# Even mixer of a hybrid encoder: when queries, keys and weight splits are asked for

## The chip, the cores and the metric

The kernel runs on one core of one Trainium2 chip. The metric is the device time of one execution in microseconds (us). Before the change three runs gave 937.4, 937.48 and 937.48 us, median 937.48.

## What is computed

The reference is a bidirectional encoder of two layers over 256 tokens (a grid of 4 rows of 64) with 1024 channels, all in float32. Each layer adds half a SwiGLU feed-forward (1024 to 2816 and back), then a mixer, then half a second feed-forward; a last RMSNorm ends it. The change lies in the mixer of the even layer:

```python
def even_mixer(h, w_in, q_gain, k_gain, sink, w_out, rope1, rope_axial):
    proj = h @ w_in            # 1024 -> qa 512, ka 128, va 128, qb 512, kb 128, vb 128
    ...
    qa = apply_axial_rope(rms_norm(qa, q_gain), *rope_axial)
    ka = apply_axial_rope(rms_norm(ka, k_gain), *rope_axial)
    oa = global_gqa(qa, ka, va)
    qb = apply_rope(qb, *rope1)
    kb = apply_rope(kb, *rope1)
    ob = windowed_gqa_sink(qb, kb, vb, sink)
    return jnp.concatenate([oa, ob], axis=-1) @ w_out
```

Group a is 8 global heads with 2 key heads, whose queries and keys are RMS-normalised per head; group b is 8 windowed heads (128 tokens to each side) with 2 key heads and a sink logit per head. A head has 64 channels.

## The kernel before, in words

**Products in split float32.** TensorE multiplies in a reduced float format (FP32R). To keep precision the kernel writes each factor as a high and a low part. ScalarE rounds a value to its high part (`high_part`, L482), VectorE subtracts it from the value for the low part (`low_part`, L485), and a product of a 128 x 128 block of activations with a 128 x 512 piece of weights is three matmuls: high by high (L474), high by low (L475) and low by high (L476). Weights come from HBM as raw tiles through SyncE's DMA queue (L382); a raw tile is cut into splits of two pieces each.

**What sets the order.** Every engine runs its instructions in the order in which the program issues them. The program counts in products: after each one it calls `tick`. A tick first issues the low part of the piece whose high part was issued last (`low`), then advances the tasks, in the order in which they were started, and last adds the stage's rate to the counter `due`; when `due` reaches the size of the next split step (1 for this stage's narrow pieces, 2 for the wide pieces of the feed-forward), that high part is issued (`supply`) and the size is taken off. A product whose piece isn't split yet has it split on the spot, high and low (`mm`). A task is a Python generator: `yield n` means that it goes on n ticks later. All the lists of waits and rates at the head of the file are such counts. `EVEN_RATE` gives 0.38, 0.48, 0.48, 0.48 and 0.5 pieces per product for the five parts of the even mixer. `due` is set anew only near the end of each feed-forward (`ENDS`).

**The even mixer** works on two blocks of 128 tokens (`tt` 0 and 1) and has 80 products: 16 for keys and values of both groups, 16 for group b's queries, 16 for group a's queries, and 16 for each half of the output projection, b first. In each part block 0 has the first eight. It uses 40 narrow pieces, eight per part, each for both blocks.

**Keys** (`keys`): a tick after a block's projection ScalarE copies keys and values out of PSUM; group a's keys are normalised on VectorE and GpSimd; GpSimd rotates them; `KB_WAIT` ticks later TensorE transposes them (L1206) into a bank of the pool `tp`, which has two; a tick later ScalarE takes their high part (kTaz, kTbz), and another tick later VectorE the low part (kTax, kTbx, beside a copy of the high part on GpSimd, L594).

**Queries** (`queries`): a tick after the projection VectorE rotates them out of PSUM (L1142 or L1144, then L1157); for group b three ticks later (`ROPE_WAIT`), for group a nine ticks later (`QA_WAIT`), TensorE transposes them (L552) into a `tp` bank; a tick later `stack_q` issues the two halves' high parts on ScalarE, and another tick later their low parts on VectorE. The odd layer's mixer calls `stack_q` too.

**Attention** (`attend`): one task goes through the head pairs of group b, then of group a. It starts a pair when the query task of its block and the key tasks have ended. A pair issues its scores on TensorE at once (L1068, L1069, and for group b L1072, a mask), and later, by `EVEN_WAITS`, the row maximum on VectorE, the exponentials on ScalarE (L1108), sum and reciprocal on VectorE, the scaling on GpSimd (L1122), transposes (L1130) and the product with the values (L1053) on TensorE. Until the first pair starts the task asks in each tick; between pairs it waits `EVEN_GAP` ticks.

Of the kernel before, what the change touches and what calls it, by code (L numbers as in the profile page):

```python
# [62 lines left out]
NAT_WAIT = 2  # L63
ROPE_WAIT = [3, 3]
KB_WAIT = {
    "a": [8, 7],
    "b": [8, 9],
}
KA_WAITS = [[1, 6], [0, 5]]
QA_WAIT = [9, 9]  # L70
ROWS, ROWS_WAIT = 4, 30
BIAS_WAIT, BIAS_GAP = 4, [0, 3]
EVEN_GAP = {
# [135 lines left out]
class Trunk:  # L209
# [88 lines left out]
    def plan(self):  # L298
# [65 lines left out]

        yield from ffn("ffn1", 0, 0)
        yield from even()
        yield from ffn("ffn2", 0, 2)
        yield from ffn("ffn1", 1, 3)
# [204 lines left out]
        self.low_part(flat(lo), tb[:, : n * P], flat(hi))  # L573
        dest += [(hi[:, i, :], lo[:, i, :]) for i in range(n)]

    def stack_q(self, tb, tag, bufs, dest):


        X = [self.t([P, 4 * P], f"{tag}{s}", bufs, F32R) for s in range(2)]
        for s in range(2):  # L580
            self.high_part(X[s][HALF[s]], tb[HALF[s]])
        yield 1
        for s in range(2):
            self.low_part(X[s][HALF[1 - s]], tb[HALF[s]], X[s][HALF[s]])
        dest += [[X[s][:, b * P : b * P + P] for s in range(2)] for b in range(4)]
# [587 lines left out]
    def even(self, sink):  # L1173
        nc = self.nc
        rates = iter(EVEN_RATE)
        flat = lambda t: t.rearrange("p a b -> p (a b)")
        tab = {
            "a": [[self.gtab[:, tt, i, :] for i in range(4)] for tt in range(NT)],
            "b": [[self.tab[:, tt, i, :] for i in (4, 5, 2, 3)] for tt in range(NT)],
        }  # L1180
        axial = {"a": 2, "b": 1}
        kT = {g: self.keys_tiles([P, T], f"kT{g}") for g in "ab"}
        vv = {g: [self.t([P, P], f"v{g}{tt}") for tt in range(NT)] for g in "ab"}
        qT = {g: [[], []] for g in "ab"}
        oT = {g: [[], []] for g in "ab"}
        by = [None, None]
        made = {"a": [], "b": []}

        def keys(g, tt, ps):
            yield 1  # L1190
            r = self.rstd_of(tt)
            o = 256 if g == "b" else 0
            k = self.t([P, 2, HD], f"k{g}", 2)
            kr = self.t([P, 2, HD], f"kr{g}", 2)
            nc.scalar.activation(flat(k), ps[:, o : o + P], AF.Copy, scale=r)
            nc.scalar.activation(vv[g][tt], ps[:, o + P : o + 2 * P], AF.Copy, scale=r)
            if g == "a":
                sq = self.squares(k, 2, 1.0)
                yield KA_WAITS[tt][0]
                n = self.head_rstd(sq, 2)  # L1200
                nc.gpsimd.tensor_tensor(k, k, n.unsqueeze(2).to_broadcast([P, 2, HD]), op=ALU.mult)
                yield KA_WAITS[tt][1]
            self.rope(nc.gpsimd, kr, k, 2, axial[g], *tab[g][tt][2:])
            yield KB_WAIT[g][tt]
            tb = self.bank("tp")
            nc.tensor.transpose(tb[:, :P], flat(kr), self.ident)  # L1206
            yield 1
            at = slice(tt * P, tt * P + P)
            yield from self.stack_k(tb[:, :P], *([t[:, at] for t in tiles] for tiles in kT[g]))

        def queries(g, tt, ps):
            yield 1
            r = self.now.r[tt]
            x = ps.rearrange("p (a b) -> p a b", a=8)
            qr = self.t([P, 4, 2, HD], "qr", 2)
            if g == "a":

                sq = self.squares(x, 8, r)
                self.rope(nc.vector, qr, x, 8, axial[g], *tab[g][tt][:2])
                yield QA_WAIT[tt]  # L1220
                n = self.head_rstd(sq, 8)
                by[tt] = self.little([P, 8], f"by{tt}")
                nc.gpsimd.tensor_scalar(by[tt], n, r, 1.0, op0=ALU.mult, op1=ALU.mult)
            else:
                self.rope(nc.vector, qr, x, 8, axial[g], *tab[g][tt][:2], r)
                yield ROPE_WAIT[tt]
            tb = self.turned(qr.rearrange("p j s d -> p (j s d)"))
            yield 1
            yield from self.stack_q(tb, f"qT{g}{tt}", 1, qT[g][tt])

        def heads(g):
            return self.attend(
                lambda tt: qT[g][tt],
                lambda tt, b0: len(made[g]) > 2 + tt and all(task[1] is None for task in made[g][: 3 + tt]),
                lambda b: kT[g],
                lambda b, s, kc: vv[g][kc][:, s * HD : s * HD + HD],
                lambda: True,
                f"oT{g}",
                oT[g],
                EVEN_GAP[g],  # L1240
                EVEN_WAITS[g],
                nc.gpsimd,
                sink=sink if g == "b" else None,
                scale=(lambda tt, b, s: by[tt][:, s * 4 + b : s * 4 + b + 2]) if g == "a" else None,
            )

        def both():
            yield from heads("b")
            yield from heads("a")


        self.rate = next(rates)
        W = self.take(KD)
        for tt in range(NT):
            ps = self.project(self.ready(tt), W, "s")
            for g in "ba":
                made[g].append(self.start(keys(g, tt, ps)))
        attention = None
        for g in "ba":
            self.rate = next(rates)  # L1260
            W = self.take(KD)
            for tt in range(NT):
                ps = self.project(self.now.hT[tt], W, "pj")
                made[g].append(self.start(queries(g, tt, ps)))
                if attention is None:
                    attention = self.start(both())
        self.out_proj([oT["b"], oT["a"]], attention, rates)
# [311 lines left out]
```

## Time and profile before

The profile is one execution, taken by the hardware profiler.

| | before |
|---|---|
| median of 3 runs | 937.48 us |
| the profiled execution's own time | 937.71 us |
| its span in the trace | 935.5 us |
| TensorE (PE) busy | 921.9 us (99%), 4405 matmuls |
| VectorE (DVE) busy | 773.4 us (83%) |
| ScalarE (ACT) busy | 675.4 us (72%) |
| GpSimd (POOL) busy | 92.5 us (10%) |
| DMA | 183.14 MB, mean 196 GB/s |

How to read a row of a timeline: start in us, duration in us, engine, line of the program, operation, tile written <- tiles read, shape of what is written and read, and how many instructions were merged (x3). In brackets stands the idle time of the engine just before, if any, and what ended it. PEld is the loading of weights into TensorE, which overlaps its matmuls. In this stage `tp` is a bank for transposes, `pj` one for projections, `s` one for scores; `raw` are weights, `hi` and `lo` their parts; `kra` and `krb` are rotated keys, `qr` rotated queries, `qTa` and `qTb` their transposed parts, `th` and `tl` the parts of the transposed activations.

### The profile page before, as it was taken

Reading aid. Unit: us, or ns where it says so; the run is one execution under the profiler, and the core shown is the slowest. Engines: PE = TensorE matmul, PEld = TensorE weight load, DVE = VectorE, ACT = ScalarE, POOL = GpSimd, SP = SyncE. Lnnn points to the kernel's source line nnn. Section 1 sums busy time; section 2 is a strip of 40 time slices with the busy share of each in tenths; the row PEclk is TensorE's granted clock in tenths of the full one; section 3 lists DMA queues with packets and bytes.
Section 4 is the critical chain, followed back from the end, with each engine's and each line's share of the span. In section 5 each row is a group of like instructions: output and inputs, shape, how many; then the busy total and the mean of one; then the engine's idle time right before and its main releaser. Section 6 shows DMA issues by size and latency. Waiting matters only on the chain.

```text
span 935.5 us, 12377 instructions
## 1 busy us (share of the span) xinstructions
PE 921.9 (99%) x4405; PEld 754.6 (81%) x4405; DVE 773.4 (83%) x1198; ACT 675.4 (72%) x1084; POOL 92.5 (10%) x152
## 2 busy tenths in 40 slices
PE   9999999999999999999999999999999999999997
PEld 6887888877778888888788888888878888888885
DVE  6799679778868889798988888978867696977998
ACT  7678876467777778875657879647777586778853
POOL 1300000064420000000100000008030000000001
PEclk9999999999999999999999999999999999999999
DMA  8858865654327577865466787666424367588651
GB/s 298 281 172 258 245 211 189 212 149 105 108 92 240 179 221 237 254 208 208 159 206 199 225 265 220 224 212 192 162 96 156 110 201 227 166 263 252 167 212 54
DMA packets 129341, 183.14 MB, mean 196 GB/s; under 512 B 50688, under 2 KB 63744, under 8 KB 129280
## 3 DMA queue, kind: packets, MB, share of 16 engines
q1 hardware_dynamic: 128704, 181.58, 61.6%
q10 hardware_dynamic: 576, 0.79, 0.2%
q8 instruction: 34, 0.56, 0.2%
q14 instruction: 27, 0.22, 0.1%
HBM read 169.76 MB, written 1.05 MB: 183 GB/s over the span
## 4 chain that ended last, share of the span: by engine, by line
PE 85%; DVE 8%; ACT 4%; issue 2%; DMA 1%; POOL 0%; POOLq 0%; ACTq 0%; DVEq 0%
PE s L475 12%; PE s L476 12%; PE s L474 12%; PE pj L474 11%; PE pj L475 11%; PE pj L476 11%; DVE lo L485 3%; PE o L475 2%; PE o L474 2%; PE o L476 2%; PE o L1053 2%; PE tp L1130 1%; ACT hi L482 1%; PE tp L530 1%; ACT shi L482 1%
## 5 line engine op out<-in xcount | busy, mean ns | idle before, releaser
L485 DVE TENSOR_TENSOR lo<-raw,hi 128x1024 fp32r<-128x1024 f32 (+1 forms) x372 | 377.9, 1034 | 83.6 <-ACT hi L482 81.8
L482 ACT ACTIVATE hi<-raw 128x1024 fp32r<-128x1024 f32 (+1 forms) x372 | 320.2, 892 | 54.0 <-PE pj L476 11.8
L474 PE MATMUL s<-hi,th 128*128 128x512 f32 x378 | 148.2, 392 | 0.0
L475 PE MATMUL s<-lo,th 128*128 128x512 f32 x378 | 147.4, 390 | 0.1
L476 PE MATMUL s<-hi,tl 128*128 128x512 f32 x378 | 147.3, 390 | 0.0
L474 PE MATMUL pj<-hi,th 128*128 128x512 f32 x366 | 146.2, 400 | 0.0
L475 PE MATMUL pj<-lo,th 128*128 128x512 f32 x366 | 143.3, 392 | 0.6 <-DVE lo L485 0.4
L476 PE MATMUL pj<-hi,tl 128*128 128x512 f32 x366 | 142.9, 390 | 0.0
L475 PEld LDWEIGHTS s<-lo,th 128*128 128x128 f32 x378 | 71.0, 188 | 15.0 <-DVE lo L485 0.7
L476 PEld LDWEIGHTS s<-hi,tl 128*128 128x128 f32 x378 | 71.0, 188 | 14.9
L474 PEld LDWEIGHTS s<-hi,th 128*128 128x128 f32 x378 | 71.1, 188 | 14.4
L475 PEld LDWEIGHTS pj<-lo,th 128*128 128x128 f32 x366 | 68.9, 188 | 15.1 <-DVE lo L485 2.6
L476 PEld LDWEIGHTS pj<-hi,tl 128*128 128x128 f32 x366 | 68.7, 188 | 14.5
L474 PEld LDWEIGHTS pj<-hi,th 128*128 128x128 f32 x366 | 68.9, 188 | 14.1 <-issue 1.0
L494 POOL TENSOR_TENSOR rstd<-var,mhalf 128x1 f32<-128x1 f32 (+2 forms) x16 | 17.1, 1070 | 588.3 <-ACT th L515 309.6
L563 ACT COPY turned<-glu 128x1024 uint16<-128x1024 uint16 (+1 forms) x48 | 60.1, 1252 | 11.5 <-DMA glu<-turned 11.5
L559 ACT COPY turned<-glu 128x1024 uint16<-128x1024 uint16 (+1 forms) x48 | 46.3, 965 | 23.6 <-DVE glu L797 15.6
L482 ACT ACTIVATE shi<-raw 128x1024 fp32r<-128x1024 f32 x28 | 29.7, 1059 | 40.1 <-DVE raw L398 21.3
L474 PE MATMUL s<-hi,g_h 128*128 128x512 f32 (+1 forms) x134 | 52.5, 392 | 0.0
L476 PE MATMUL s<-hi,g_l 128*128 128x512 f32 (+1 forms) x134 | 52.0, 388 | 0.0
L475 PE MATMUL s<-lo,g_h 128*128 128x512 f32 (+1 forms) x134 | 51.9, 388 | 0.0
L482 ACT ACTIVATE shi<-two 128x1024 fp32r<-128x1024 f32 x28 | 29.6, 1057 | 20.9 <-DVE two L398 20.9
(350 smaller groups left out, 1658.1 us busy)
## 6 DMA issues: line engine op xcount, KB each, us to landing
raw<-in_ffn_w_down SPq DMA_DIRECT2D x44, 1024.0 KB, 5.1
raw<-in_ffn_w_up SPq DMA_DIRECT2D x28, 1024.0 KB, 5.2
raw<-in_ffn_w_gate SPq DMA_DIRECT2D x26, 1024.0 KB, 5.2
raw<-in_ffn_w_gate SPq DMA_DIRECT2D x35, 512.0 KB, 4.1
raw<-in_ffn_w_up SPq DMA_DIRECT2D x32, 512.0 KB, 5.3
raw<-in_odd_w_qkv SPq DMA_DIRECT2D x12, 1024.0 KB, 5.2
raw<-in_even_w_in SPq DMA_DIRECT2D x4, 1024.0 KB, 5.0
raw<-in_even_w_out SPq DMA_DIRECT2D x8, 512.0 KB, 5.8
```

Source lines behind the costliest of these rows:

```text
L474: mm(ps, h, wh, start=first, stop=False)
L475: mm(ps, h, wl, start=False, stop=False)
L476: mm(ps, l, wh, start=False, stop=last)
L482: self.nc.scalar.activation(hi, src, AF.Copy)
L485: self.nc.vector.tensor_tensor(lo, src, hi.bitcast(F32), op=ALU.subtract)
L494: nc.gpsimd.tensor_tensor(r[:, :n], v[:, :n], self.mhalf[:, :n], op=ALU.pow)
L530: nc.tensor.transpose(tb[:, j * P : (j + 1) * P], self.x[tt][:, b * P : (b + 1) * P], self.ident)
L559: self.nc.scalar.copy(planes.rearrange("p (h c) -> p h c", h=2), back.rearrange("p (c h) -> p h c", h=2))
L563: self.nc.scalar.copy(planes.rearrange("p (c h) -> p h c", h=2), back.rearrange("p (h c) -> p h c", h=2))
L1053: self.nc.tensor.matmul(O[64 * s : 64 * s + 64, i * P : i * P + P], v(b0 + i, s, kc), pT[s][:, i, kc, :], start=(kc == 0), stop=(kc == 1),)
L1130: nc.tensor.transpose(tb[:, o : o + P], p[:, i, kc * P : kc * P + P], self.ident)
```

## The change

Three things change, all in the even mixer.

- `KB_WAIT["a"][0]` goes from 8 to 6: the transposes of the first block's normalised keys are issued behind the sixth product of group b's queries rather than behind the eighth.
- `stack_q` gets an argument for the wait between high and low part. The even mixer's queries pass 0, so both parts are issued in one tick, for both groups and both blocks, and the query task ends one tick sooner. The odd layer keeps the wait of 1.
- Ahead of the first product of group b's queries 2 is taken off `due`, so that two pieces' splits are withheld there.

```diff
@@ -63,11 +63,12 @@
 KB_WAIT = {
-    "a": [8, 7],
+    "a": [6, 7],
     "b": [8, 9],
 }
 KA_WAITS = [[1, 6], [0, 5]]
 QA_WAIT = [9, 9]
+Q_HOLD = 2
@@ -573,13 +574,14 @@
-    def stack_q(self, tb, tag, bufs, dest):
+    def stack_q(self, tb, tag, bufs, dest, wait=1):
 
         X = [self.t([P, 4 * P], f"{tag}{s}", bufs, F32R) for s in range(2)]
         for s in range(2):
             self.high_part(X[s][HALF[s]], tb[HALF[s]])
-        yield 1
+        if wait:
+            yield wait
         for s in range(2):
             self.low_part(X[s][HALF[1 - s]], tb[HALF[s]], X[s][HALF[s]])
@@ -1226,7 +1228,7 @@
-            yield from self.stack_q(tb, f"qT{g}{tt}", 1, qT[g][tt])
+            yield from self.stack_q(tb, f"qT{g}{tt}", 1, qT[g][tt], 0)
@@ -1260,6 +1262,8 @@
             for tt in range(NT):
+                if g == "b" and tt == 0:
+                    self.due -= Q_HOLD
                 ps = self.project(self.now.hT[tt], W, "pj")
                 made[g].append(self.start(queries(g, tt, ps)))
```

## The prediction, made before the change was timed

> **What bounds the kernel now.** I read the page first, then TensorE's waits by stretch, then the timelines of TensorE, VectorE, ScalarE and GpSimd from 160 to 300 us.
>
> ```profile
> span 935.5 us, 12377 instructions
> PE 921.9 (99%) x4405; PEld 754.6 (81%) x4405; DVE 773.4 (83%) x1198; ACT 675.4 (72%) x1084; POOL 92.5 (10%) x152
> ```
>
> TensorE is idle for only 935.5 - 921.9 = 13.6 us. What a change can give is some of these waits; what it can take is any new wait of TensorE, which nothing later gives back. The stage around the edit, the even mixer, holds three waits that matter. I name its products (three matmuls each) by order: q0 to q15 project the windowed heads' queries, a0 to a15 the global heads' queries, w0 to w15 and v0 to v15 are the two halves of the output projection, f0 on are the next feed-forward's gates. S0 to S7 are the windowed heads' score groups. First wait: the transposes of the queries of the first 128 tokens (L552), behind q11.
>
> ```profile
> 207.46 0.63 PE L552 MATMUL tp<-mats,qr 128*128 128x128 f32 x4 [0.69 <-DVE kTax L485]
> ```
> ```profile
> 202.00 2.19 DVE L485 TENSOR_TENSOR lo<-raw,hi 128x512 fp32r<-128x512 f32 x3
> 204.21 1.53 DVE L1144 SCALAR_TENSOR_TENSOR t<-pj,rstd,tab 128x512 f32<-128x512 f32 x3
> 205.78 1.03 DVE L1157 TENSOR_TENSOR qr<-t,t 128x256 f32<-128x256 f32 x2
> 206.73 0.58 DVE L485 TENSOR_TENSOR kTax<-tp,kTaz 64x128 fp32r<-64x128 f32 x2
> 207.34 0.70 DVE L485 TENSOR_TENSOR lo<-raw,hi 128x512 fp32r<-128x512 f32 x1
> 208.07 0.59 DVE L485 TENSOR_TENSOR kTbx<-tp,kTbz 64x128 fp32r<-64x128 f32 x2
> 208.69 0.69 DVE L485 TENSOR_TENSOR lo<-raw,hi 128x512 fp32r<-128x512 f32 x1
> 209.41 1.41 DVE L485 TENSOR_TENSOR qTb<-tp,qTb 64x512 fp32r<-64x512 f32 x2
> ```
>
> VectorE's queue is the cause: the rotated queries (qr) are done at 206.81, but their transposes need the bank that kTax reads until 207.31, and kTax stands behind the rotation. Second wait, 0.57 us at S0 for the queries' low part; third, 0.94 us at S4:
>
> ```profile
> 207.84 0.47 PE L474 MATMUL pj<-hi,th 128*128 128x512 f32 x1
> ...
> 208.61 0.40 PE L474 MATMUL pj<-hi,th 128*128 128x512 f32 x1
> ...
> 209.30 0.27 PE L1206 MATMUL tp<-mats,kra 128*128 128x128 f32 x1
> 210.15 0.39 PE L1068 MATMUL s<-kTbz,qTb 128*128 128x256 f32 x1 [0.57 <-DVE qTb L485]
> ...
> 221.34 0.36 PE L1068 MATMUL s<-kTbz,qTb 128*128 128x256 f32 x1 [0.94 <-ACT p L1108]
> ```
> ```profile
> 219.78 0.69 DVE L485 TENSOR_TENSOR lo<-raw,hi 128x512 fp32r<-128x512 f32 x1 [0.19 <-ACT hi L482]
> 220.50 1.41 DVE L485 TENSOR_TENSOR qTb<-tp,qTb 64x512 fp32r<-64x512 f32 x2
> ```
>
> The last row's first half (0.69 to 0.70) ends at 221.2, so S4 waits for the second query block's low part as much as for the named exponentials. All three waits together are 2.20 us: that is the ceiling of any gain, 0.23%, just over the 0.2% (1.9 us) that a measurement of this kernel can tell from no change.
>
> **The change part by part.** *The withheld splits* are the part that reaches furthest, so first how far ahead of need the weights are split. The narrow weight pieces of this stage (hi on ScalarE, lo on VectorE) number 40, eight for each of keys and values, q, a, w and v. ScalarE has done 15 of them by q0, the last three here, and the 40th here:
>
> ```profile
> 194.13 1.72 ACT L482 ACTIVATE hi<-raw 128x512 fp32r<-128x512 f32 x3
> ...
> 263.10 0.62 ACT L482 ACTIVATE hi<-raw 128x512 fp32r<-128x512 f32 x1
> ```
>
> With 0.48 due per product (0.5 in v), and the order of hi among ScalarE's other instructions, the remaining 25 are asked for behind q1, q3, ... q15, a1, a4, a6, ... a14, w0, w2, ... w10, w13, w15, v1, v3; no other starting remainder than 0.28 to 0.40 gives that order. Taking 2 from the due drops q1 and q3 and leaves all other places, so from then on each place serves the piece two further back. The counter is not refilled before the next feed-forward's end. Today a piece comes four products or more ahead of its use in the tight spots. After, the list of needs meets the list of places so: the last piece of a (a7) comes behind a6; the pieces of w2, w3 and w7 behind w0, w2 and w6; that of v2 behind v1; and v3's would come behind v3 itself, so the product asks for it on the spot. The work of one piece, hi then lo, is about 1.3 us (0.62 and 0.69 by the rows above) against 0.69 for a product (208.61 to 209.30), so a lead of one or two products is not enough when ScalarE or VectorE has something else in its queue. What it costs goes by the times at which these places now deliver, since both engines are led by TensorE's attention work there:
>
> ```profile
> 222.22 0.67 DVE L485 TENSOR_TENSOR lo<-raw,hi 128x512 fp32r<-128x512 f32 x1
> ...
> 239.40 0.69 DVE L485 TENSOR_TENSOR lo<-raw,hi 128x512 fp32r<-128x512 f32 x1
> ...
> 241.13 0.68 DVE L485 TENSOR_TENSOR lo<-raw,hi 128x512 fp32r<-128x512 f32 x1
> ...
> 263.13 0.69 DVE L485 TENSOR_TENSOR lo<-raw,hi 128x512 fp32r<-128x512 f32 x1
> ...
> 280.03 1.22 DVE L485 TENSOR_TENSOR lo<-raw,hi 128x1024 fp32r<-128x1024 f32 x1
> ...
> 283.06 1.23 DVE L485 TENSOR_TENSOR lo<-raw,hi 128x1024 fp32r<-128x1024 f32 x1
> ```
> ```profile
> 222.36 0.39 PE L475 MATMUL pj<-lo,th 128*128 128x512 f32 x1
> ...
> 239.13 0.39 PE L475 MATMUL pj<-lo,oTb00h 128*128 128x512 f32 x1
> ...
> 240.26 0.39 PE L475 MATMUL pj<-lo,oTb00h 128*128 128x512 f32 x1
> ...
> 263.28 0.39 PE L475 MATMUL pj<-lo,oTa00h 128*128 128x512 f32 x1
> ...
> 280.23 0.39 PE L475 MATMUL s<-lo,th 128*128 128x512 f32 x1
> ...
> 282.05 0.39 PE L475 MATMUL s<-lo,th 128*128 128x512 f32 x1
> ```
>
> These are the second matmuls of a7, w2, w3, v3, f4 and f6, which read lo.
> - a7: its lo would end at 222.89, 0.53 after the need. +0.6 (0 if the shift of VectorE's queue hides it, 1.2 if a6 waits too).
> - w2 and w3: 240.09 against 239.13 is 0.96; 241.81 against 240.26 is 1.55, the larger, which contains the first. For the global heads' queries the low part (1.41 by the row of the same shape) now also moves ahead of w3's lo. +2.0, between 0.2 (VectorE ahead by its two withheld lo, 1.4) and 3.0 (1.55 + 1.41). w7 is then covered by that delay.
> - v2 and v3: the lo behind v1 ends at 263.82; v3's own, asked for on the spot, follows it with 0.7, so 264.5 against 263.28, 1.2; a head's low part may stand between. +1.5, between 0.3 and 2.5.
> - f: v3's extra call catches up one unit of due, the other stays missing, so the wide pieces come about one place late: f4's lo where now the 280.03 row is, f6's where the 283.06 row is, ending at 281.25 and 284.29 against 280.23 and 282.05, that is 1.0 and 2.2. +1.7, between 0.5 and 2.4.
>
> What withholding gives: two lo of the row with x3 (0.73 each) no longer stand ahead of the rotation at 204.21. But q7, whose result the rotation reads, ends no sooner than the transpose behind it now starts:
>
> ```profile
> 203.62 0.27 PE L1206 MATMUL tp<-mats,kra 128*128 128x128 f32 x1
> ```
>
> And the next lo, whose hi now stands behind the keys' kTaz on ScalarE (the transpose two products of 0.69 ahead of 203.62, at 202.3, then kTaz to about 203.1 and hi to 203.7), ends near 204.4. So I let the rotation start at 204.4, not sooner than today. *The keys' transposes*, two products earlier, put kTax ahead of the rotation too; nothing stands behind it that is harmed, its 0.58 fits into VectorE's freed time, and q6 and q7 only move behind a transpose that was on TensorE anyway. GpSimd's two kTax copies move along. Together: qr ends at 204.4 + 2.6 = 207.0, the transposes start at 207.1 in place of 207.46. -0.35 (between -0.69 and 0).
>
> On GpSimd there is a rule to weigh. VectorE's lo took 0.73 each at 202.0, and 0.65 here, where GpSimd has nothing to do:
>
> ```profile
> 171.69 1.29 DVE L485 TENSOR_TENSOR lo<-raw,hi 128x512 fp32r<-128x512 f32 x2 [2.07 <-ACT hi L482]
> ```
>
> The Trainium skill, "SBUF — State Buffer", Who interferes with whom, says that a VectorE instruction with two SBUF inputs contends with a GpSimd instruction that reads SBUF, and that the second to issue is blocked until the first is done. By it the moved copies could hold back the lo ahead of the rotation by a whole copy and the gain of 0.35 would be gone; the rows show 0.08 per instruction, and the sum goes by them.
>
> *The low part right behind the high part* takes away one product's wait, and with it the query task ends one product earlier, so S0 is queued behind q12 and no longer behind q13 and the keys' transpose. TensorE takes its queue in order, and so q13 now stands behind the wait. From the transposes' start T: TensorE reaches S0 at T + 1.15 (208.61 - 207.46). VectorE has 0.70 + 0.59 + 0.69 ahead of the low part from 207.0 on, so it starts near 209.0 and its first half ends near 209.7 = T + 2.6. The wait is 1.45 in place of 0.57: +0.9 (between +0.3, if VectorE is free when ScalarE is done, and +1.2). At S4 the low part no longer stands behind the 219.78 lo, which gives up to 0.72; but S4 itself comes one product earlier, ahead of a6, and the first softmax's sum and reciprocal now stand ahead of the second query block's rotation and wait for ScalarE. I take -0.2 (between -0.75 and +0.3).
>
> Sum: -0.35 + 0.9 - 0.2 + 0.6 + 2.0 + 1.5 + 1.7 = +6.15. The profiled execution took 937.71, of which 2.2 lie around its span; the median of the runs is 937.48. So 937.48 + 6.15 = 943.6.
>
> **The rivals.**
> *Not slower (935.3 to 936.4).* The late pieces cost nothing, because without the two splits ScalarE and VectorE run 1.4 us ahead and keep that: then a7, w, v and f are all within reach, the first wait goes by 0.35 and S4's by 0.72, and S0's extra wait stays near zero. 937.5 - 1.1 = 936.4; with all three waits gone, 2.2, 935.3. It decides if the lo of w0's place ends before 239.1. Against it: VectorE has idle time in this stage at several places (it waits on ScalarE and TensorE), and each such gap wipes out a lead.
> *No change (937.5 to 938.5).* The late pieces cost about what the waits give back: a deficit that VectorE takes up in stages where it is idle. Against it stands that v3's piece is asked for on the spot in any case.
> *Much slower (949 and above).* The missing unit stays to the end of the next feed-forward, where seven-product stages have their own tight places: some three more waits of 1 us, and all terms at their upper ends (11 us). For it: there TensorE has hardly any wait now, so I cannot see the margins. Against: the rates there are higher than the need, so a deficit shrinks.
>
> **How the numbers follow.** Forecast (slower by 1.9 to 11 us) 0.77; not slower 0.08; no change 0.08; much slower 0.07. The range takes in the bounds of the forecast and the upper half of the no-change case, and leaves out 0.08 + 0.04 + 0.07 = 0.19: 938.0 to 948.5. Faster by over 0.2% (under 935.6) is half of the not-slower case, 0.04; within 0.2% is its other half and the no-change case, 0.12; slower 0.84.
>
> **What would show it.** The 0.69 wait at L552 should shrink to about 0.35; S0's wait at L1068 should grow to about 1.4; TensorE should show new waits for lo and hi (L475, L474) in the stretches 222, 239 to 242, 262 to 266 and 278 to 285, about 5 to 7 us together, and its idle time should rise from 13.6 to near 20. If those lo waits are absent, the central step is wrong. If S0's wait falls instead, the order argument is.

## The result and the profile after

The changed kernel takes 951.82 us (median of 4 runs, 951.67 to 952.92); four runs of the kernel before beside it give 937.44 (937.2 to 937.48). The ratio is 1.0155, 95% interval 1.0143 to 1.0167: slower by 14.4 us, where 6.15 was forecast. The profiled execution took 951.92 us. The head of its page:

```profile
span 950.0 us, 12381 instructions
...
PE 927.0 (98%) x4405; PEld 755.7 (80%) x4405; DVE 773.5 (81%) x1198; ACT 675.5 (71%) x1084; POOL 88.9 (9%) x152
```

TensorE is idle for 950.0 - 927.0 = 23.0 us, 9.4 more than before, and although the same 4405 matmuls run, it is "busy" for 5.1 us more. So only two thirds of the loss stand in the brackets of its waits. These are its waits in the stage (lines in this kernel count one more above `stack_q` and two more below it):

```profile
207.09 0.63 PE L553 MATMUL tp<-mats,qr 128*128 128x128 f32 x4 [0.34 <-DVE qr L1159]
...
209.72 0.39 PE L1070 MATMUL s<-kTbz,qTb 128*128 128x256 f32 x1 [1.31 <-DVE qTb L486]
...
221.06 0.39 PE L1070 MATMUL s<-kTbz,qTb 128*128 128x256 f32 x1 [0.96 <-DVE qTb L486]
...
222.77 0.50 PE L476 MATMUL pj<-lo,th 128*128 128x512 f32 x1 [0.49 <-DVE lo L486]
...
241.02 0.47 PE L475 MATMUL pj<-hi,oTb00h 128*128 128x512 f32 x1 [0.68 <-DVE t L1144]
242.32 0.51 PE L476 MATMUL pj<-lo,oTb00h 128*128 128x512 f32 x1 [0.83 <-DVE lo L486]
...
245.60 0.80 PE L476 MATMUL pj<-lo,oTb00h 128*128 128x512 f32 x1 [2.32 <-DVE lo L486]
246.19 0.63 PE L477 MATMUL pj<-hi,oTb00l 128*128 128x512 f32 x1
246.75 1.98 PE L1055 MATMUL o<-pt,vb 128*64 128x128 f32 x16
...
259.11 0.39 PE L1070 MATMUL s<-kTaz,qTa 128*128 128x256 f32 x1 [0.63 <-ACT p L1110]
268.42 0.50 PE L477 MATMUL pj<-hi,oTa00l 128*128 128x512 f32 x1 [0.83 <-DVE oTa00l L486]
272.49 0.50 PE L476 MATMUL pj<-lo,oTa00h 128*128 128x512 f32 x1 [0.57 <-DVE lo L486]
...
290.37 0.50 PE L476 MATMUL s<-lo,th 128*128 128x512 f32 x1 [0.38 <-DVE lo L486]
290.71 0.39 PE L477 MATMUL s<-hi,tl 128*128 128x512 f32 x1
```

In order: the first wait is halved (0.69 to 0.34), S0's has grown (0.57 to 1.31), S4's is the same, and then come new waits for low parts of weights: at a6, ahead of which S4 now stands, at w2, w3 (2.32), v2 and f2. Smaller ones, which this list leaves out, follow at v3 (0.22), v7 (0.44), f4 (0.23) and f6 (0.45 for a high part, 0.76 for a low one). The waits for parts of weights add up to 6.7 us in brackets, within the 5 to 7 that the prediction gave as its sign, yet the loss is 14.4. The 16 products with the values at 246.75 take 1.98 us; such a row took 1.09 before (at 236.22). The three rows from 245.60 on last 1.6 to 1.8 times as long as such rows elsewhere in the list: TensorE's clock has fallen (0.50 from 244.47 on, as the last section shows).

The ledger by stretches uses the windows view: window, its length, then for PE, PEld, DVE, ACT and POOL the busy time and (x instructions), the granted clock, the DMA share and GB/s. The windows run from the first matmul of q0, a0, w0, v0 and f0 to the next mark, the last to f16. Before:

```profile
198.04:213.00 14.96, 13.70 (x70) 10.76 (x68) 12.40 (x27) 9.76 (x24) 10.07 (x25) 1.00 0.61 149
213.00:235.43 22.43, 21.48 (x146) 17.11 (x146) 19.55 (x52) 17.64 (x54) 10.80 (x23) 1.00 0.44 100
235.43:258.29 22.86, 22.66 (x158) 18.23 (x156) 19.97 (x46) 16.54 (x43) 9.02 (x15) 1.00 0.29 95
258.29:276.83 18.54, 18.31 (x126) 14.21 (x126) 10.52 (x27) 15.27 (x42) 4.08 (x9) 1.00 0.30 95
276.83:288.65 11.82, 11.82 (x57) 9.81 (x56) 10.90 (x24) 10.79 (x20) 1.69 (x2) 1.00 0.36 122
```

After:

```profile
198.03:213.46 15.43, 13.78 (x69) 10.78 (x68) 11.14 (x25) 8.92 (x22) 8.97 (x26) 1.00 0.35 89
213.46:237.84 24.38, 22.93 (x165) 18.21 (x164) 19.53 (x54) 18.68 (x60) 9.89 (x21) 1.00 0.38 87
237.84:266.87 29.03, 24.47 (x139) 18.83 (x138) 19.33 (x43) 14.96 (x37) 9.05 (x14) 0.88 0.33 88
266.87:288.25 21.38, 19.19 (x127) 14.08 (x126) 11.44 (x29) 15.38 (x43) 4.52 (x9) 1.00 0.23 80
288.25:302.99 14.74, 12.92 (x58) 9.74 (x56) 12.49 (x25) 10.93 (x20) 0.74 (x2) 1.00 0.43 142
```

The lengths differ by 0.47, 1.95, 6.17, 2.84 and 2.92, together 14.35, which is the whole loss. One correction: w0 now has 16 products with the values ahead of it that stood behind it before (x146 to x165, x158 to x139), since the attention runs one product earlier. They are worth about 1.3 us: with the low part alone moved (e2_low below) TensorE is busy for 1.27 us less in the third stretch. So a0 to w0 costs about 0.7 and w0 to v0 about 7.4. That stretch, where 2.0 was forecast, is where the prediction failed.

Why does w3 wait so long? VectorE's timeline in the changed kernel:

```profile
241.58 0.69 DVE L486 TENSOR_TENSOR lo<-raw,hi 128x512 fp32r<-128x512 f32 x1
...
243.43 1.39 DVE L486 TENSOR_TENSOR qTa<-tp,qTa 64x512 fp32r<-64x512 f32 x2
244.85 0.69 DVE L486 TENSOR_TENSOR lo<-raw,hi 128x512 fp32r<-128x512 f32 x1
```

The piece of w2 ends at 242.27 and that of w3 at 245.54; ahead of the second stand the global heads' low parts, which the change moved one tick forward.

### The profile page after: what moved, and what is told of

Read it like the earlier page. It is cut to its first block, busy times and chain, and to the rows that moved or that the text cites. A ratio compares the mean times of both kernels' runs of the same rounds, so it can differ in the third digit from the quotient of the medians.

```text
span 950.0 us, 12381 instructions
## 1 busy us (share of the span) xinstructions
PE 927.0 (98%) x4405; PEld 755.7 (80%) x4405; DVE 773.5 (81%) x1198; ACT 675.5 (71%) x1084; POOL 88.9 (9%) x152
## 4 chain that ended last, share of the span: by engine, by line
PE 82%; DVE 9%; ACT 5%; issue 2%; DMA 0%; POOL 0%; POOLq 0%; ACTq 0%; DVEq 0%
PE s L476 12%; PE s L477 12%; PE s L475 12%; PE pj L476 11%; PE pj L477 11%; PE pj L475 11%; DVE lo L486 4%; PE o L475 2%; PE o L476 2%; PE o L477 2%; ACT hi L483 2%; PE o L1055 2%; PE tp L1132 1%; ACT shi L483 1%; PE tp L476 1%
```

## The experiments

The main theory was the prediction's: the withheld splits cost what the low parts of weights are late, wherever the lead is short. The rivals were that the scores, asked for a product too early, cause most of it; that it is the order of w3's piece and the global queries' low part on VectorE; and that the clock's fall at w3 is a large part. Where shifts are given, a product's start is counted from that of q0 in the same profiled execution, and compared with the kernel before; that leaves out what happens ahead of the stage. Runs of the kernel before vary from 937.25 to 941.72 us on the chips of the experiments; part of this comes from the clock, in the last section.

### The hold alone (e1_hold)

```diff
+Q_HOLD = 2
...
+                if g == "b" and tt == 0:
+                    self.due -= Q_HOLD
```

> Only the two splits are withheld; keys and queries as before. Theory (late pieces): every later place serves a piece two further back, so new waits for lo stand at a7, w2, w3, v2, v3 and at the start of the next feed-forward, and the time is 3.5 to 6.5 us above before. Rival (early scores): the hold itself is nearly free, under 1 us, because the 14.4 us come from the scores that stand one product earlier. Clock at 1.0 in the stage, if no cluster of waits is as dense as the one around w2 and w3 of the changed kernel.

947.21 against 939.06, ratio 1.0089 (1.0067 to 1.011), more than the 3.5 to 6.5 us expected. The shift at f16 is 7.4 us: -0.6 to a0, +0.35 to w0, +2.36 to v0, +2.33 to f0, +2.92 to f16. TensorE's waits between w0 and v4:

```profile
240.38 0.50 PE L476 MATMUL pj<-lo,oTb00h 128*128 128x512 f32 x1 [0.83 <-DVE lo L486]
242.10 0.50 PE L476 MATMUL pj<-lo,oTb00h 128*128 128x512 f32 x1 [0.32 <-DVE lo L486]
246.81 0.50 PE L476 MATMUL pj<-lo,oTb02h 128*128 128x512 f32 x1 [0.47 <-DVE lo L486]
...
266.51 0.50 PE L476 MATMUL pj<-lo,oTa00h 128*128 128x512 f32 x1 [1.16 <-DVE lo L486]
```

The hold by itself is half of the loss. Its waits come at a7, w2, w3 and v2, which the prediction named, but also at a6 (0.22), at w7 (the 0.47 above), which was to be covered, and at v7 (0.43), and in f at f2 as well as at f4 and f6; v3 has none. The three waits in w add to 1.62 us in brackets and to 2.36 in the shift. The first wait is nearly gone here; VectorE's rotation and TensorE's transposes:

```profile
204.27 1.53 DVE L1145 SCALAR_TENSOR_TENSOR t<-pj,rstd,tab 128x512 f32<-128x512 f32 x3 [1.62 <-PE pj L477]
```
```profile
207.35 0.63 PE L553 MATMUL tp<-mats,qr 128*128 128x128 f32 x4
```

The matmul ahead of them ends at 207.22, so 0.13 us are left of the 0.69, with the keys' transposes at their old place.

### The low part alone (e2_low)

```diff
-        yield 1
+        if wait:
+            yield wait
...
-            yield from self.stack_q(tb, f"qT{g}{tt}", 1, qT[g][tt])
+            yield from self.stack_q(tb, f"qT{g}{tt}", 1, qT[g][tt], 0)
```

> Only the queries' low part right behind the high part; no splits withheld, keys' transposes as before. Theory (late pieces): S0 waits about 1.3 in place of 0.57 and S4 about as before, the order behind shifts by a product: 1 to 2.5 us above before, no waits for lo of weights. Rival (early scores): 8 us or more above before, with the dense waits around w2 and w3 and the halved clock still there.

943.91 (ratio 1.0041, 1.0022 to 1.006); shift 3.0 at f16, above the 1 to 2.5 us expected and far from the rival's 8. No wait for a weight's low part is left. S0 waits 1.37 us, S4 0.96; w2 waits 0.68 for the rotation that still reads its bank, the global scores 0.62 for exponentials, and v 0.82 for a head's low part. These are the 0.68, 0.63 and 0.83 of the changed kernel, so they belong to this edit.

### The hold paid back (e3_paid)

```diff
+                if g == "a":
+                    self.due += Q_HOLD / 2
```

> The changed kernel, but one piece each is given back to the due ahead of each block's first product of the global heads' queries. Theory (late pieces): what hurts is that the deficit is never paid back, so the lo waits of w, v and the feed-forward's start vanish, the clock stays at 1.0, and 1 to 3 us above before remain from the early scores. Rival (the hold hurts where it stands, in q and early a): 8 us or more above before remain.

On the changed kernel: 942.62 (1.004, 1.0026 to 1.0055), shift 3.8 at f16, a little above the 1 to 3 us expected. All waits for the weights' low parts are gone, and the shift is 0.8 above that of the low part alone. What costs is not that two splits are late at q, but that the counter never returns to where it was.

### The clock kept up at w3 (e4_warm)

The changed kernel with 14 matmuls whose result nobody reads, put between the first two matmuls of w3:

```diff
+        if self.fill:
+            spare = self.bank("o")
+            for _ in range(self.fill):
+                self.nc.tensor.matmul(spare[:, : 3 * P], self.ident16, self.m16[:, : 3 * P], start=True, stop=True)
+            self.fill = 0
...
+                            if self.now.n == 1 and (g, tt, nh, k) == (0, 0, 1, 1):
+                                self.fill = 14
```

> The changed kernel with 14 extra matmuls of 384 columns between the first and the second matmul of w3, into a bank that nobody reads, so that TensorE works through most of the 2.32 us wait there. They add work that the result doesn't need. Theory (clock): the granted clock stays at 1.0 after it, and the time falls by 2.5 to 3.5 us against the changed kernel, to about 948.8, though 14 matmuls are added. Rival (the halved clock costs nothing, or does not come from idleness): no change, or slower by the extra matmuls, 951.8 to 953.

TensorE's timeline at the fillers and behind them:

```profile
245.99 2.45 PE L480 MATMUL o<-m 128*128 128x384 bf16 x14
248.47 0.50 PE L482 MATMUL pj<-lo,oTb00h 128*128 128x512 f32 x1
...
249.13 1.09 PE L1061 MATMUL o<-pt,vb 128*64 128x128 f32 x16
```

The clock holds at w3: the 16 products take 1.09 again, and w2 to v0 grows by 4.3 us in place of 6.4, though the fillers last a little longer than the wait. But in this execution the clock fell for 3.4 us at 224.6 instead, behind the waits of S4 and a6, and the total is 952.1 (1.0142, 1.0125 to 1.016), not the 948.8 expected. So the clock's share at w3 is shown, about 2.1 us; that fillers save it overall is not.

### The changed kernel again (e5_again)

> The changed kernel once more, beside the others on one chip. Theory (late pieces, early scores and the clock gate): 13 to 15 us above before, with one or two stretches of 3.4 us at half clock in the even mixer, not always at the same product, since the waits only make the stage idle enough and where the clock falls depends on where its window stands. Rival (the clock falls because of one certain wait, at w3): always right behind w3.

952.63 (1.0154, 1.0136 to 1.0173), with all the waits of the first profile to within 0.02 us. The clock fell for 3.4 us behind w3, not for 6.8, and once more at 464.9, outside the stage. So in both executions it fell behind w3, and it is e4_warm, not this run, that speaks against the rival. The window from w0 to v0 took 1.0 us less than in the first profile, all of it busy time:

```profile
238.18:266.18 28.00, 23.42 (x140) 18.14 (x137) 19.34 (x43) 14.97 (x37) 9.06 (x14) 0.94 0.35 87
```

### Low part at once, scores not earlier (e6_late)

On the kernel before, the low part at once, but the query task ends at its old tick:

```diff
+        if not wait:
+            yield 1
```

> Only the low part right behind the high part, but the query task ends one product later as before, so the scores keep their places on TensorE; no splits withheld, keys as before. Theory (it is the early scores that cost): S0 waits 0.6 as before, S4 waits less than 0.94, and the time is within 1 us of before. Rival (VectorE's order costs, the low parts ahead of other work): 2 to 4 us above before, as with the low part alone.

939.35 (1.0016, 1.0004 to 1.0028), shift 1.4 us at f16; the runs stay just within the 1 us expected. S0's wait is back at 0.57, and S4's is gone. But two other waits are new in TensorE's timeline:

```profile
223.90 0.89 PE L1134 MATMUL tp<-mats,p 128*128 128x128 f32 x4 [1.07 <-POOL p L1126]
...
243.41 1.09 PE L1057 MATMUL o<-pt,vb 128*64 128x128 f32 x16 [1.20 <-DVE oTb10l L486]
```

With the scores kept at their place 1.6 of the low part's 3.0 us are gone. The low part itself helps at S4; what is left of its cost goes by these two waits, for GpSimd's scaling and for a head's low part.

### The keys alone (e7_keys), and keys with the hold paid back (e8_hold_paid)

The first has only `"a": [6, 7]` in `KB_WAIT`; the second adds the hold and its repayment, and leaves the low part where it was.

> Only the keys' transposes two products earlier. Theory: VectorE's work ahead of the queries' transposes is the same, only in another order, so the wait of 0.69 there stays between 0.5 and 0.7, now for the rotated queries and not for the bank, and the time is within 0.5 us of before. Rival (the bank alone was the cause): the wait shrinks to about 0.1 and the time falls by 0.6 us.

> Keys' transposes earlier, two splits withheld and given back one each ahead of the global heads' two query blocks, the low part one product behind the high part as before. Theory (early scores cost, and an unpaid deficit): the first wait shrinks to 0.35, S0 waits about 0.6, S4 as before or 0.3 more where the paid back pieces stand in front, and the time is between 0.5 below and 1.2 above before. Rival (withholding costs even when paid back): 3 us or more above before.

Keys alone: 938.05 (1.0005, 0.9992 to 1.0018). The wait at the transposes goes from the bank to the rotated queries, 0.87 us, longer than the 0.5 to 0.7 expected. With the hold it falls to 0.33: 938.78 (1.0002, 0.999 to 1.0014). But e1_hold, with the hold and the keys at their old place, has 0.13 there: it is the hold that shrinks this wait, and the keys' move costs some 0.2 us with the hold and without it (shift at a0 -0.40 against -0.56, and +0.17 against 0). With the counter repaid the two edits neither gain nor lose in the runs; in the trace the shift at f16 is +0.7.

### The global queries' low part a tick later (e9_a_apart)

```diff
-            yield from self.stack_q(tb, f"qT{g}{tt}", 1, qT[g][tt], 0)
+            yield from self.stack_q(tb, f"qT{g}{tt}", 1, qT[g][tt], int(g == "a"))
```

> The changed kernel, but the global heads' queries keep one product between high and low part; the windowed heads' have none. Theory: in the changed kernel their low part (1.4 us) stands on VectorE ahead of the piece that w3 needs, so w3's wait falls from 2.32 to between 0.3 and 1.0, the clock is not halved at w3, and the time is 2 to 5 us under the changed kernel (947 to 950). Rival (w3's wait is the missing lead alone): w3 waits 2 us or more and the time is within 1 us of the changed kernel.

w3's wait in TensorE's timeline, and the window from w0 to v0:

```profile
244.56 0.50 PE L476 MATMUL pj<-lo,oTb00h 128*128 128x512 f32 x1 [0.78 <-DVE lo L486]
```

```profile
238.36:263.53 25.17, 21.99 (x139) 16.89 (x138) 19.19 (x43) 14.97 (x37) 9.26 (x14) 1.00 0.37 96
```

w3 waits 0.78 in place of 2.32 and the clock does not fall there: w0 to v0 takes 25.17 us, 3.86 less than in the changed kernel, of which 1.38 is idle time and 2.48 busy time. With the 1.27 us of moved products put back the stretch costs 3.6 us against the kernel before, as much as hold (2.36) and low part (1.28) add up to when each is alone: what the two cost together beyond that is gone. The time is 950.47 (1.0128, 1.0112 to 1.0143), just above the 947 to 950 expected and less of a gain than 3.86; in the profiled execution the clock fell later, at 464.1, behind a wait of 3.0 us for the residual (1.6 before), where the shift grows by 2.9 us again.

### A version of the low part that might pay (e10_scores), and with the hold (e11_scores_hold)

On the kernel before: only the windowed heads' low part at once, the task's end kept, and in `EVEN_WAITS["b"]` the third list goes from [1, 3, 2, 1] to [1, 3, 3, 0], so that GpSimd's scaling has a product more ahead of its transposes, where e6_late waits 1.07. The second kernel adds the keys and the repaid hold.

```diff
+        if not wait:
+            yield 1
...
-            yield from self.stack_q(tb, f"qT{g}{tt}", 1, qT[g][tt])
+            yield from self.stack_q(tb, f"qT{g}{tt}", 1, qT[g][tt], int(g == "a"))
```

> From the kernel before: only the windowed heads' low part right behind the high part, the query task ends a product later as before, and the third pair's transposes of probabilities come one product later (3 and 0 for 2 and 1). Theory: S4's wait of 0.94 goes, and the 1.07 us wait that came at those transposes in its place goes too, since a product more stands ahead of them: 0.4 to 1.2 us under before. Rival (the wait moves on once more, to the next pair): within 0.3 us of before.

> The run before this one, with the keys' transposes two products earlier and two splits withheld and given back ahead of the global heads' query blocks. Theory: the first wait falls by 0.35 as well, and what the given back pieces cost at S4 is hidden by the earlier low part: 0.5 to 1.5 us under before. Rival (pieces given back delay VectorE by as much): 0 to 1 us above before.

The two waits that e10_scores has left, in TensorE's timeline:

```profile
207.43 0.63 PE L553 MATMUL tp<-mats,qr 128*128 128x128 f32 x4 [0.66 <-DVE kTax L486]
...
210.12 0.39 PE L1072 MATMUL s<-kTbz,qTb 128*128 128x256 f32 x1 [0.58 <-DVE qTb L486]
```

The other waits of the stage are of 0.23 us, as before, and 0.17: S4's is gone. 937.03 against 938.88, ratio 0.9979 (0.9971 to 0.9988), the only version ahead of the kernel before. The trace shows 0.7 us of it, from the wait at S4, and the fastest runs differ by 0.85 (936.43 against 937.28). By the mean granted clock of each run the clock fell less often here: it is 0.997 or less in 1 of 11 runs, and in 10 of 21 of the kernel before. But among the other runs the means still differ by 1.4 us, so about half of that stays open. With keys and hold the same kernel gives 938.67 (1.0001, 0.999 to 1.0011), not the gain of 0.5 to 1.5 expected: the first wait shrinks to 0.34, but new ones at a7 (0.43) and w2 (0.32) take it back, and its shift at f16 is -0.2.

### A hold of one (e12_hold1)

As e1_hold, with 1 in place of 2:

```diff
+Q_HOLD = 1
```

> Only one split withheld, never given back; keys and queries as before. Theory (lead): with one piece fewer ahead the places of a, w2 and w3 still hold, v3 and the next feed-forward's start do not; 2.5 to 5 us above before, most of it behind v2. Rival (cost in proportion): half of what two cost, 4 us, spread over a, w, v and the feed-forward's start.

942.51 (1.004, 1.0026 to 1.0054). The shift is -0.5 at v2 and then +1.3 at v8, +1.1 at f0, +4.0 at f16: no wait for a weight's part at a or w, waits at v3 (0.43) and v7 (0.44), and the same four in f as with a hold of two. The total is about half of what two cost, so it alone would not tell the theory from the rival; the places do. The loss comes where the lead runs out, all of it behind v2, and is not spread in proportion.

## Why the prediction was wrong

The direction held, and so did the main mechanism, low parts of weights that come late; the places held in part, and one step failed. The steps against the runs:

| step | forecast | measured | single edits |
|---|---|---|---|
| first wait and S0 (q0 to a0) | +0.55 | +0.47 | hold -0.57, low +0.90, keys +0.16 |
| S4 and a7, the latter at a6 (a0 to w0) | +0.4 | +0.7 | hold +0.35, low +0.35 |
| w2 and w3 (w0 to v0) | +2.0 | +7.4 | hold +2.36, low +1.28 |
| v (v0 to f0) | +1.5 | +2.84 | hold +2.33, low +0.43 |
| f (f0 to f16) | +1.7 | +2.92 | hold +2.92, low 0 |

In the second and third rows 1.27 us of moved products are put back, in the column of the low part too; by the busy time of a0 to w0 in e2_low (23.07 against 21.48) it would be up to 1.6, so the split between these two rows is good to some 0.3 us. In every row but the third the parts alone add to the whole; there they give 3.6, and 3.8 us exist only together.

- **The first wait, S0.** The sizes came out: 0.34 and 1.31 us, where 0.35 and 1.45 were expected. For the first wait part of that is luck. The prediction let the rotation start no sooner than in the kernel before and counted on the keys' move. With the hold alone the rotation starts 5.77 us behind q0 (204.27 in e1_hold), where it took 6.17 before, and the wait is 0.13. With the keys moved too, kTax and one more low part stand ahead of it, it starts 6.49 behind q0, and the wait is 0.34. The copies on GpSimd did no harm: the low part just ahead of the rotation (203.81) took 0.69 us. The 0.08 per instruction that the prediction read is a mean over merged rows; one by one, the three instructions of its 202.00 row take 0.69, 0.89 and 0.77, and one without GpSimd at work takes 0.68 to 0.69.
- **S4.** The forecast said a gain of 0.2, and named why it would not be 0.75. There was none. VectorE's timeline in the changed kernel shows the first softmax in the way:

```profile
215.23 0.16 DVE L1119 TENSOR_TENSOR tot<-sums,es 128x2 f32<-128x2 f32 x1 [0.82 <-ACT es L1023]
...
215.51 1.52 DVE L1146 SCALAR_TENSOR_TENSOR t<-pj,rstd,tab 128x512 f32<-128x512 f32 x3
```

VectorE waits 0.82 us for ScalarE with the second block's rotation queued behind. e10_scores, where the scores keep their place, shows the gain that was given up.
- **w2 and w3, the step that failed.** Its term was +2.0, and 7.4 was measured. Its range ended at 3.0, the case in which the global queries' low part does stand ahead of w3's piece. That case came in full (e9_a_apart) and the sum should have been made with it: the two waits are 0.83 + 2.32 = 3.15 us. Not in the step at all were the bank wait at w2 (0.68) and the exponentials (0.63), both there with the low part alone, and the halved clock, 2.5 us by the busy time of the changed kernel against e9_a_apart (24.47 - 21.99). These three and the lo waits are 6.96 us; the other 0.5 is less than what four restarts behind waits would cost by the next point (1.0), so this row is closed to about half a us.
- **v and f: mis-sized.** The steps took the end of the late piece less its need, for the last piece alone. In v the two places forecast show only 0.57 (v2) and 0.22 (v3) in brackets; a wait at v7 (0.44), and at v0 the 0.83 for a head's low part (0.23 before), which comes with the low part alone, were not in the sum. In f the waits are at f2, f4 and f6, the first not forecast, and their brackets, 1.82, are near the term of 1.7. But the price of a wait is more than its bracket. In the changed kernel's rows of f2, the first matmul of the product starts at 289.61 and the second at 290.37, 0.76 apart where back-to-back rows are 0.23 apart (288.93, 289.15, 289.38), so 0.53 for a bracket of 0.38: rows overlap by 0.16, which a wait undoes. The third starts 0.34 behind the second, another 0.11. Each wait costs about 0.26 us more than it shows; the four in f are 1.82 in brackets and 2.92 in the shift. That is the gap in f.
- **The rivals.** "Not slower" is refuted by its own point: w2's low part ends at 242.27, not before 239.1. Its condition, that the late pieces cost nothing, needs at least the counter repaid: then the waits for weights' low parts are gone (e3_paid, e8_hold_paid), though neither kernel is faster than before. "Much slower" has the right size, for one of its two reasons: the terms of w, v and f did come out above their upper ends. The other did not hold: behind f16 no wait for a low part came in that feed-forward, and the next 120 products add 0.4 us, so the deficit does not last through it.

The account closes: hold 7.4, low part 3.0 and keys 0.2 alone, order at w3 1.4 (idle time, changed kernel against e9_a_apart) and the clock 2.5, together 14.5 against 14.4 at f16. The interaction is what the method missed: each late piece was priced against the engines' times of the kernel before, as if the other edits left them alone.

## What to carry to other kernels

Where splits are issued by a count, taking a few off was nearly free here (0.7 us in the trace) only with the count repaid before the first tight place, and cost 7.4 without; find that place by listing needs against places of issue through to where the counter is set anew. Price a new wait by start to start, not by its bracket, and price two edits that load the same in-order queue together, at the upper end if both can stand ahead of one need. Where new waits of a few us fall close together on TensorE, add the cost of its clock: here 2.5 us for 6.8 us at half clock, and 1.4 to 1.6 for 3.4 us (busy time of w0 to v0 in e5_again against e9_a_apart, of a0 to w0 in e4_warm against the changed kernel).

## What the runs showed of the hardware

TensorE's clock was halved in the middle of the kernel without a single window of full idleness. Windows of 3.4 us just before and from the fall on, changed kernel, columns as above:

```profile
241.06:244.47 3.41, 1.39 (x4) 0.60 (x4) 3.33 (x8) 1.19 (x3) 0.99 (x1) 1.00 0.61 126
244.47:251.30 6.83, 5.70 (x24) 4.23 (x25) 2.16 (x4) 1.94 (x4) 1.12 (x2) 0.50 0.00 0
```

The late fall in e9_a_apart, and a window of the kernel before at the same place, which was followed by none:

```profile
460.70:464.10 3.40, 0.79 (x6) 0.75 (x7) 3.15 (x5) 0.10 (x1) 0.00 (x0) 1.00 0.89 295
464.10:467.50 3.40, 3.40 (x10) 2.65 (x9) 1.82 (x5) 2.38 (x8) 0.00 (x0) 0.50 0.06 21
```
```profile
447.40:450.80 3.40, 1.77 (x11) 1.23 (x10) 3.38 (x5) 0.00 (x0) 0.00 (x0) 1.00 0.84 288
```

TensorE was busy for 1.39 of 3.41 us (41%) and 0.79 of 3.40 (23%) ahead of the two falls, and for 52% where none followed. In the middle of the fourteen traces all eight windows of this grid with 44% or less were followed by a fall, and of the thirteen from 52 to 60% one (57%, ahead of 224.6 in e4_warm), so the bound isn't sharp. The half-speed stretches in mid-kernel last 3.413 us or twice that, and begin a whole number of such windows after the start of the first stretch at full clock (238.93 us, 70 windows, in both profiles of the changed kernel). Which wait is caught, and whether one or two windows follow, therefore varies with where the windows lie: at w3 for 6.8 us and 3.4 us in two executions of one kernel, at 224.6 in e4_warm. The Trainium skill, "TensorE: Matmul & The Clock Gate", Part 1: The HAM clock gate, gives such a free-running window of 3413 ns, which agrees, and lets the clock drop after one idle window; here a window that was less than half busy was enough.

The end of the next feed-forward, where TensorE waits 1.4 to 3.0 us for the residual (L530), lies at this edge, and the clock fell there in six of the fourteen profiled executions. In these six the shift grows by 1.9 to 2.9 us across that wait, in the others it changes by -0.2 to +0.7. Over the 58 runs of the kernel before beside the experiments, those with a mean clock of 0.997 or less take 939.8 us on average and the others 938.4. So the clock is one cause of the spread, and edits below 2 us are better compared by their shifts within the stage too.
